# Output projection of a hybrid decoder block: eight half-size block products become seven, with block sums of rows and weights made on chip

## The chip, the cores and the metric

The kernel runs on one core of one Trainium2 chip. The metric is the device time of one execution in microseconds (us); lower is better. The engines are PE (matrix products, with PEld for the loading of its weights), DVE (vector), ACT (scalar, with the activation functions), POOL (GpSimd) and SP (which issues the DMA transfers). DVE and ACT read and write both memories on chip, SBUF and PSUM; POOL works on SBUF alone here; PE writes PSUM.

## What is computed

One layer of a decoder block on x of 1024 rows (sequence) by 1024 columns (model width), in float32:

```
h  = RMSNorm(x);  p = h @ w_in        # split into q, k, v, latents, gate_a, gate_b
A  = sliding-window attention          B = latent attention, causal
y  = sigmoid(gate_a) * (A @ w_o_swa) + sigmoid(gate_b) * (B @ w_o_mla)
x  = x + y @ w_out                     # the output projection: 1024 x 1024 by 1024 x 1024
h  = RMSNorm(x, ffn_norm_g)
x  = x + (silu(h @ w_gate) * (h @ w_up)) @ w_down
return RMSNorm(x, final_norm_g)
```

## The kernel before

**Precision.** Each factor of a product is split into a high part in the rounded matmul format fp32r and a low part, the rest. `split` (line 161) makes them: ACT copies to the high part (line 163), DVE subtracts it from the source (line 166). `mm3` (line 168) then issues three matmuls for each block of 128 of the inner dimension: high x high, high x low, low x high (lines 172, 173, 174), 512 columns wide, into one PSUM bank.

**Block products.** The gates (`gates`, 8 pairs of weight columns), the feed-forward's first products (`ffn`) and its last one already use seven products of half-size blocks instead of eight (class `Seven`, line 710): sums of blocks of both factors are made first, and the seven results are added up in two groups of PSUM banks, A (products 1, 2, then 5, 3) and B (6, 7, 4). `prep_to(n)` (line 784) converts weights up to the n-th product of the list, `run` (line 789) issues one product, after it has called prep_to for as many ahead as `n_ahead` says. The output projection still is eight half-size products, one after the other.

**Sliding-window stage** (lines 1025 to 1042). Sixteen iterations of attention are interleaved with the gates' products, three a piece: `gate_step`, transposes of q (`sw_qT`), `gate_step`, `sw_pv`, `sw_scores` of the next iteration (score products, maxima on DVE, exponentials on ACT), `gate_step`, `sw_pT`. The order on all engines is the order of the program here.

**Latent attention** (line 1360 on) carries in its slots the products A @ w_o_swa (`mix_a`, line 1276): result rows `ar`, in blocks dc of 128 of the model width. Those of dc 0 to 3 go out to memory (`ar_d`), those of dc 4 to 7 stay on chip.

**Mixing** (`mix_b`, line 1411, called from the loop at line 1444). For each dc in the order DCS = (4, 5, 0, 1, 6, 7, 2, 3) and each half of the sequence (`sh`, 512 columns): 12 matmuls with w_o_mla into a bank `oB`; DVE multiplies by the sigmoid of gate b (line 1420) and adds the product of gate a and `ar` that POOL made (lines 1434, 1426); `split` writes the row's parts into `quad` (`yh`, `yl`). y is held transposed: a block dc of it is 128 of the inner dimension of the next product. The loads and conversions of w_o_mla (`ob`) and of w_out (`out`) are set into the loop by hand through the list `st` (`load_to`, `conv_to`).

**Projection** (lines 1611 to 1652). Four segments (half of the sequence, half of the columns): (0,0), (0,1), (1,1), (1,0). In each, four row blocks b of 128; for each b 24 matmuls (8 blocks of the inner dimension in the order DCS, three each) into a bank `xo`, and DVE adds the bank to x (line 1629). When a row block is complete in both halves of the columns, its norm follows: Square with a sum on ACT (line 1635), mean and power on POOL (lines 311, 314), scaling on DVE (line 1640), and one block later `to_h` (line 1468): 8 transposes on PE and the block differences that the feed-forward's seven products need (for b 0 to 3 the blocks b11, b21; for b 4 to 7 t2, t3, b22, and later t1, t4, on DVE). The w_out weights of the third segment are loaded and converted anew, 12 units of 128 x 1024 in all.

**Feed-forward start** (lines 1653 to 1676). Eight products (q 1 and 2 of two pairs, for gate and up weights) need only b11 and b21; the ninth needs t2 of all four late row blocks.

**What sets the order.** Inside `tc.manual_schedule(...)` the named engines keep the order of the program. From line 1043 to the fourth segment of the projection no engine is held: there the framework orders each engine's instructions when the program is built, by their place in the program and by what it reckons to be ready; an instruction can be moved ahead of earlier ones that wait. From the fourth segment on (line 1613) PE, DVE, ACT and POOL are held. At run time each engine works strictly in its order. On-chip buffers are two pools: 21 of 4 KB a partition (`U`) and 17 of 8 KB (`V`); PSUM has 8 banks, 4 for `P1` and 4 for `PX`. A tile waits until a buffer of its pool is free.

## Time and profile before

| | |
|---|---|
| time, median of 3 runs | 1345.6 us (1345.04 to 1346.36) |
| time of the profiled execution | 1345.58 us |
| its span | 1343.8 us |
| mean granted clock of PE | 0.998 |
| DMA | 223.61 MB, mean 166 GB/s |

The profile is one execution, recorded by the hardware on the one core. Its views: the page (busy time of each engine and its costliest groups of instructions), the list of waits (who waited for whom: total, times, longest), the groups of one stretch ("x16 | 16.3, 1035 | 0.6" reads: 16 instructions, 16.3 us busy, 1035 ns the mean of one, 0.6 us idle on the engine just before them), the stretches (busy time of each engine between two times) and the timeline (start, duration, engine, line, operation, what it writes <- what it reads; in brackets the idle time of the engine before it and what ended that). Times are counted from the start of the span. Matmuls are pipelined: their durations overlap, and the cost of one is the distance between starts. Line numbers are those of the kernel before.

### The profile page before, as it was taken

How to read it: one execution, taken by the hardware profiler on the slowest of the kernel's cores; microseconds unless marked ns; L12 is line 12 of the kernel's file. 1: busy time of each engine (PE TensorE's matmuls, PEld its weight loads, DVE VectorE, ACT ScalarE, POOL GpSimd, SP SyncE). 2: the span in 40 equal slices, each digit the busy share in tenths (PEclk: the TensorE clock that was granted, in tenths of full speed). 3: DMA queues.
4: the chain of work that ended last, by engine and by line, in shares of the span. 5: the costliest groups of instructions: out<-in, count | busy, mean ns of one | idle time of the engine just before them, and what ended most of it. 6: DMA issues, size and time to landing. Idle time of an engine off the chain costs nothing. (4 is left out here: it accounts for less than half of the span.)

```text
span 1343.8 us, 19035 instructions
## 1 busy us (share of the span) xinstructions
PE 1325.5 (99%) x6564; PEld 1115.0 (83%) x6564; DVE 903.5 (67%) x1471; ACT 635.7 (47%) x1291; POOL 567.6 (42%) x614
## 2 busy tenths in 40 slices
...
GB/s 374 152 188 156 118 97 83 109 124 187 155 243 160 107 99 17 264 268 48 190 140 96 166 175 146 203 162 180 177 141 153 164 96 194 383 373 238 173 13 144
DMA packets 85311, 223.61 MB, mean 166 GB/s; under 512 B 9632, under 2 KB 16288, under 8 KB 84128
## 3 DMA queue, kind: packets, MB, share of 16 engines
...
q8 instruction: 52, 0.85, 0.3%
...
## 5 line engine op out<-in xcount | busy, mean ns | idle before, releaser
L166 DVE TENSOR_TENSOR wl<-wr,wl 128x512 fp32r<-128x512 f32 x150 | 150.8, 1029 | 72.6 <-ACT wl L163 72.2
L166 DVE TENSOR_TENSOR lrv<-lr,lrv 128x1024 fp32r<-128x1024 f32 x77 | 105.1, 1396 | 49.3 <-ACT lrv L163 45.3
L163 ACT CAST lrv<-lr 128x1024 fp32r<-128x1024 f32 x77 | 80.1, 1052 | 95.7 <-PE fd L174 69.8
L172 PE MATMUL fd<-lrv 128*128 128x512 f32 x308 | 119.8, 389 | 0.0
L173 PE MATMUL fd<-lrv 128*128 128x512 f32 x308 | 119.8, 389 | 0.0
L174 PE MATMUL fd<-lrv 128*128 128x512 f32 x308 | 119.8, 389 | 0.0
L177 POOL TENSOR_TENSOR wr<-wr,sm 128x512 f32<-128x512 f32 (+1 forms) x38 | 46.2, 1225 | 145.4 <-DVE wl L166 114.2
L163 ACT CAST wl<-wr 128x512 fp32r<-128x512 f32 x150 | 86.9, 622 | 1.9 <-DVE wr L835 1.7
L1198 POOL TENSOR_TENSOR denb<-denb,neg_one 128x1 f32<-128x1 f32 x64 | 40.1, 626 | 96.2 <-ACT p L1197 84.1
L166 DVE TENSOR_TENSOR wl<-sm,wl 128x512 fp32r<-128x512 f32 x60 | 48.7, 837 | 46.3 <-ACT wl L163 46.2
L311 POOL TENSOR_SCALAR ms<-ss 128x1 f32<-128x1 f32 x32 | 9.4, 292 | 143.7 <-ACT xn L1635 67.5
L173 PEld LDWEIGHTS fd<-lrv 128*128 128x128 f32 x308 | 57.8, 188 | 12.1
L174 PEld LDWEIGHTS fd<-lrv 128*128 128x128 f32 x308 | 57.8, 188 | 12.0
L172 PEld LDWEIGHTS fd<-lrv 128*128 128x128 f32 x308 | 57.8, 188 | 11.9
L1197 ACT ACTIVATE p<-scb,nmb 128x384 f32<-128x384 f32 (+3 forms) x64 | 47.8, 747 | 33.3 <-DVE nmb L1196 25.6
L166 DVE TENSOR_TENSOR ptl<-pTb,pth 128x512 fp32r<-128x512 f32 (+2 forms) x96 | 50.5, 552 | 16.6 <-ACT pth L163 16.3
L1196 DVE CUSTOM_DVE_ANT_0 scb<-scb,mask 128x384 f32<-128x384 f32 (+3 forms) x64 | 48.6, 761 | 15.0 <-PE scb L1188 13.0
L1529 ACT ACTIVATE act<-sm 128x512 f32<-128x512 f32 x11 | 7.0, 633 | 104.8 <-DVE sm L180 104.8
L1199 POOL TENSOR_SCALAR p<-p,denb 128x384 f32<-128x384 f32 (+3 forms) x64 | 47.9, 748 | 6.3
L172 PE MATMUL xo<-wv,yh 128*128 128x512 f32 x120 | 47.4, 395 | 1.2 <-ACT yh L163 1.2
L1529 ACT ACTIVATE act<-pu 128x512 f32<-128x512 f32 x22 | 13.9, 633 | 71.0 <-DVE pu L180 71.0
L163 ACT CAST pth<-pTb 128x512 fp32r<-128x512 f32 (+2 forms) x96 | 43.4, 482 | 8.5 <-PE pTb L1213 7.5
...
## 6 DMA issues: line engine op xcount, KB each, us to landing
...
```

Of the source, the lines that this page charges most:

```text
L163: i = nc.scalar.copy(hi, src)
L166: (eng or nc.vector).tensor_tensor(lo, src, hi.bitcast(F32), op=ALU.subtract)
L172: nc.tensor.matmul(ps, ah, bh, start=first and i == 0, stop=False, skip_group_check=go_on)
L173: nc.tensor.matmul(ps, ah, bl, start=False, stop=False, skip_group_check=go_on)
L174: nc.tensor.matmul(ps, al, bh, start=False, stop=last and i == n - 1, skip_group_check=go_on)
L177: eng.tensor_tensor(out, a, b, op=ALU.subtract)
L311: nc.gpsimd.tensor_scalar(ms, ss, 1.0 / width, EPS, op0=ALU.mult, op1=ALU.add)
L1196: nc.vector.tensor_tensor_reduce(s_, s_, m_, 1.0, -NEG, op0=ALU.add, op1=ALU.min, accum_out=nm)
L1197: nc.scalar.activation(p_, s_, AF.Exp, scale=-1.0, bias=nm, accum_out=den)
L1198: nc.gpsimd.tensor_tensor(den, den, neg_one[:, 0:1], op=ALU.pow)
L1199: nc.gpsimd.tensor_scalar(p[:, 0:w], p[:, 0:w], den, 0.0, op0=ALU.mult, op1=ALU.add)
L1529: nc.scalar.activation(dst, src, AF.Silu)
```

## The change

The projection becomes seven products of half-size blocks, in the order 1, 2, 6, 5, 3, 7, 4, with four row blocks b each and 12 matmuls for each b. With y and w_out cut into 2 x 2 blocks, the sums of y blocks (`y_sums`) are made in place on POOL, those of w_out (`w_sums`) on DVE, and each product's two factors are split when their turn comes (`split_left`, `conv_out`; `left` and `wop` hold them). The mixed rows stay on chip in float32 (`ya`) until their sums are made; only the blocks that enter a product unsummed are split inside `mix_b`. Partial results are copied by ACT (p1, p5) and added to x by DVE (`xo`) and POOL (`more`). PE keeps the order of the program from the first product on, all four engines from the seventh product in the list's order (q = 7) on. The four early row blocks are normed behind product 3, the four late ones behind product 4, which ends the projection. In `to_h` three of the late blocks' subtractions move from DVE to POOL. The two halves of the model width swap roles (dc 0 to 3 for 4 to 7) in `mix_a`, `ar_d` and DCS, and the w_o_mla weights go to the `V` pool. In the sliding-window stage, two calls of `prep_to` are added ahead of `sw_scores`.

```diff
@@ -296,15 +296,10 @@
     for k in range(2):
         ukv_unit(k)
     uq_unit(2)
-    for dp in range(4):
+    for dp in (2, 3, 0, 1):
         plain(("oa", dp), w_o_swa[dp], (P, 4, 256), True)
-    for dp in (2, 0, 3, 1):
-        plain(("ob", dp), w_o_mla[dp], (P, 4, 256))
-    OUT0 = (2, 0, 3, 1)
-    for r, hf in enumerate((0, 1, 0)):
-        for j in (range(4) if r else OUT0):
-            plain(("out", r, j), w_out[hf, j], (P, 2, 512), (r, j) != (2, 3))
-
+    for dp in (0, 2, 1, 3):
+        plain(("ob", dp), w_o_mla[dp], (P, 4, 256), True)
...
@@ -1032,6 +1027,8 @@
         if it >= 1:
             sw_pv(it - 1)
         if it + 1 < N_SW:
+            if gates.seq[gates.n_run][:2] in ((2, 1), (5, 1)):
+                gates.prep_to(gates.n_run + 3)
             sw_scores(it + 1)
         if it == N_SW - 1:
...
@@ -1308,14 +1305,14 @@
     wo = {}
     NT = NH * NB
     LATE = True
-    DCS = (4, 5, 0, 1, 6, 7, 2, 3)
+    DCS = (0, 1, 4, 5, 2, 3, 6, 7)
...
@@ -1408,23 +1405,63 @@
     if not LATE:
         mix_a(*rest.pop(0), 0, 4, PX("oA"))
+    left = {}
+    ya = {}
+    def new_left(q):
+        left[q] = (V("yh", F32R), V("yl", F32R))
     def mix_b(dc, i):
         if dc % 2 == 0:
             wo[4 + dc // 2] = st.get(("ob", dc // 2))
         w = wo[4 + dc // 2]
         ga, gb = gate.pop(dc), gate.pop(8 + dc)
+        ya[dc] = ga
         for sh in range(2):
             cs = half(sh)
             pb = PX("oB")
             mm3(pb, [((w[0][:, c, blk(dc % 2)], w[1][:, c, blk(dc % 2)]), obT[(c, sh)]) for c in range(4)])
             nc.vector.tensor_tensor(gb[:, cs], pb, gb[:, cs], op=ALU.mult)
-            if i == 7:
-                add(ga[:, cs], ga[:, cs], gb[:, cs], nc.vector)
-                split(*hT(dc, cs), ga[:, cs])
-        for sh in range(2 if i < 7 else 0):
-            cs = half(sh)
             add(ga[:, cs], ga[:, cs], gb[:, cs], nc.vector)
-            split(*hT(dc, cs), ga[:, cs])
+            if dc >= 4 or sh == 0:
+                hi, lo = left[1 if dc < 4 else 2 if sh == 0 else 4]
+                split(hi[:, dc % 4], lo[:, dc % 4], ga[:, cs])
+    def y_sums(k):
+        a, b = ya[k], ya[4 + k]
+        a_lo, a_hi, b_lo, b_hi = a[:, half(0)], a[:, half(1)], b[:, half(0)], b[:, half(1)]
+        add(b_hi, a_hi, b_hi, nc.gpsimd)
+        sub(a_hi, a_lo, a_hi, nc.gpsimd)
+        sub(a_lo, b_hi, a_lo, nc.gpsimd)
+        sub(b_lo, b_lo, a_lo, nc.gpsimd)
+    S_OF = {6: (0, 0), 7: (0, 1), 3: (1, 0), 5: (1, 1)}
+    def split_left(q):
+        new_left(q)
+        kh, sh = S_OF[q]
+        for k in range(4):
+            split(left[q][0][:, k], left[q][1][:, k], ya[4 * kh + k][:, half(sh)])
+    wraw = {}
+    wop = {}
+    def load_out(kh, hf, j):
+        wraw[(kh, hf, j)] = U("wr", F32, (P, 2, 512))
+        nc.sync.dma_start(wraw[(kh, hf, j)], w_out[hf, 2 * kh + j])
+    W_OF = {1: (0, 0), 2: (1, 0), 3: (1, 1), 4: (1, 0), 5: (0, 1), 6: (0, 0), 7: (1, 1)}
+    def conv_out(q, j, eng=None):
+        wop[(q, j)] = halves_of((P, 2, 512), True)
+        split(*wop[(q, j)], wraw[(*W_OF[q], j)], eng)
+    def w_sums(j, eng):
+        b11, b12, b21, b22 = (wraw[(kh, hf, j)] for kh in range(2) for hf in range(2))
+        sub(b22, b22, b12, eng)
+        sub(b12, b12, b11, eng)
+        add(b11, b11, b22, eng)
+        sub(b21, b21, b11, eng)
...
@@ -1439,13 +1476,16 @@
     held[0] = True
     sigmoids(DCS[0])
     held[0] = False
-    st.conv_to(st.index[("ob", 0)])
-    new_quads("y")
+    st.conv_to(st.index[("ob", 2)])
+    new_left(1)
     for i, dc in enumerate(DCS):
         if i in (1, 2):
-            st.load_to(st.index[("ob", (3, 1)[i - 1])])
-        if 2 <= i < 6:
-            st.load_to(st.index[("out", 0, OUT0[i - 2])])
+            st.load_to(st.index[("ob", i * 2 - 1)])
+        if 4 <= i:
+            load_out(0 if i < 6 else 1, 0, i % 2)
+        if i == 2:
+            new_left(2)
+            new_left(4)
         if i + 2 < 8:
             load_sigs(DCS[i + 2])
         if rest:
@@ -1454,23 +1494,25 @@
             sigmoids(DCS[i + 1])
         mix_b(dc, i)
         if i in (2, 3):
-            st.conv_to(st.index[("ob", (3, 1)[i - 2])])
-        if i >= 4:
-            st.conv_to(st.index[("out", 0, OUT0[i - 4])])
+            st.conv_to(st.index[("ob", 2 * i - 3)])
+        if i in (4, 5):
+            y_sums(i - 4)
+        if i in (5, 6):
+            conv_out(1, i - 5)
     fg_bc = bcast_gain("ffng", ffn_g)
     raw1 = {}
-    x2 = {}
     late = []
     hq.clear()
+    x2 = {}
     def to_h(xn, b):
         c = b % 4
         pss = []
         for kh in range(2):
-            ps = PX("tp", (P, 4, P))
+            ps = (P1 if b < 4 else PX)("tp", (P, 4, P))
             for j in range(4):
...
@@ -1492,16 +1534,18 @@
         nc.scalar.copy(t23[:, 1], pss[0])
         sub(t23[:, 0], pss[1], r[:, 0], nc.vector)
         nc.scalar.copy(hq["t2"][0][:, :, blk(c)], t23[:, 0])
-        sub(r[:, 1], r[:, 1], t23[:, 0], nc.vector)
+        hi, lo = hq["t2"]
+        sub(lo[:, :, blk(c)], t23[:, 0], hi[:, :, blk(c)].bitcast(F32), nc.gpsimd)
+        sub(r[:, 1], r[:, 1], t23[:, 0], nc.gpsimd)
         late.append((c, r))
         def rest():
             sub(t23[:, 1], pss[1], t23[:, 1], nc.vector)
             nc.scalar.copy(hq["b22"][0][:, :, blk(c)], pss[1])
             nc.scalar.copy(hq["t3"][0][:, :, blk(c)], t23[:, 1])
-            for name, src in (("t2", t23[:, 0]), ("b22", pss[1]), ("t3", t23[:, 1])):
+            for name, src in (("b22", pss[1]), ("t3", t23[:, 1])):
                 hi, lo = hq[name]
-                sub(lo[:, :, blk(c)], src, hi[:, :, blk(c)].bitcast(F32), nc.vector)
+                sub(lo[:, :, blk(c)], src, hi[:, :, blk(c)].bitcast(F32), nc.vector if name == "b22" else nc.gpsimd)
         return rest
...
@@ -1605,64 +1649,157 @@
             split_h(name, c, r[:, i])
         late[c] = None
+    pe_order = tc.manual_schedule(engines={engines.PE})
+    pe_order.__enter__()
+    p1, p5 = V("xp1"), V("xp5")
+    lo, hi = half(0), half(1)
+    bank = {}
+    normed = {}
+    def xo(q, b):
+        if q in (1, 6, 5):
+            bank[("B" if q == 6 else "A", b)] = (PX if q == 6 else P1)("xo")
+        ps = bank[("B" if q in (6, 7, 4) else "A", b)]
+        lh, ll = left[q]
+        mm3(ps, [((lh[:, k, blk(b)], ll[:, k, blk(b)]), (wop[(q, k // 2)][0][:, k % 2], wop[(q, k // 2)][1][:, k % 2]))
+                 for k in range(4)], first=q in (1, 6, 5), go_on=q in (2, 7, 4, 3))
+        if q == 1:
+            nc.scalar.copy(p1[:, b], ps)
+        elif q == 5:
+            nc.scalar.copy(p5[:, b], ps)
+        else:
+            x_ = x2[b if q in (2, 6, 3) else 4 + b][:, {2: lo, 6: hi, 3: hi, 7: hi, 4: lo}[q]]
+            add(x_, ps, x_, nc.vector)
+    def norm_a(b):
+        xn = U("xn")
+        ss = tiny("ss")
+        nc.scalar.activation(xn, x2[b], AF.Square, accum_out=ss)
+        normed[b] = xn, rstd_of(ss, D)
+    def norm_b(b):
+        xn, rs = normed[b]
+        nc.vector.scalar_tensor_tensor(xn, x2[b], rs, fg_bc, op0=ALU.mult, op1=ALU.mult)
+        nc.sync.dma_start(x2_d[b], x2.pop(b))
+    def more(x_, p):
+        add(x_, x_, p, nc.gpsimd)
+    conv_out(2, 0)
+    conv_out(2, 1)
+    for j in range(2):
+        load_out(0, 1, j)
+        load_out(1, 1, j)
+    y_sums(2)
+    y_sums(3)
+    for b in range(4):
+        xo(1, b)
+        if b == 0:
+            w_sums(0, nc.vector)
+        if b == 1:
+            w_sums(1, nc.vector)
+        if b == 2:
+            conv_out(6, 0)
+            split_left(6)
+        if b == 3:
+            conv_out(6, 1)
+        x2[b] = load_x(b)
+    for b in range(4):
+        xo(2, b)
+        more(x2[b][:, hi], p1[:, b])
+        if b == 1:
+            conv_out(5, 0)
+            split_left(5)
+        if b == 2:
+            conv_out(5, 1)
+    for b in range(4):
+        xo(6, b)
+        if b == 0:
+            for j in range(2):
+                wraw[(0, 0, j)] = None
+                t = wraw[(0, 0, j)] = U("wr", F32, (P, 2, 512))
+                nc.sync.dma_start(t, w_out[1, 2 + j])
+            W_OF[3] = (0, 0)
+        if b == 2:
+            split_left(3)
+            conv_out(3, 0)
+        if b == 3:
+            conv_out(3, 1)
+    for b in range(4):
+        xo(5, b)
+        if b == 0:
+            split_left(7)
+            conv_out(7, 0)
+        if b == 1:
+            conv_out(7, 1)
+        x2[4 + b] = load_x(4 + b)
+        more(p5[:, b], p1[:, b])
+    for b in range(4):
+        xo(3, b)
+        more(x2[4 + b][:, hi], p5[:, b])
+        more(x2[4 + b][:, lo], p1[:, b])
+        norm_a(b)
+        norm_b(b)
+        if b == 1:
+            conv_out(4, 0)
+        if b == 2:
+            conv_out(4, 1)
+    ffn.load_part(0, 0)
+    pe_order.__exit__(None, None, None)
     in_order = tc.manual_schedule(engines={engines.PE, engines.DVE, engines.Activation, engines.Pool})
...
+    in_order.__enter__()
+    for b in range(4):
+        xo(7, b)
+        if b == 0:
+            ffn.load_part(0, 1)
+        to_h(normed.pop(b)[0], b)
+        if b == 1:
+            ffn.mix(0)
+    ffn.prep_to(3)
+    lowers = {}
+    def to_h_of(b):
+        lowers[b] = to_h(normed.pop(b)[0], b)
     ffn.n_ahead = 1
...
+    xo(4, 0)
+    norm_a(4)
+    xo(4, 1)
+    norm_a(5)
+    norm_b(4)
+    xo(4, 2)
+    norm_a(6)
+    norm_b(5)
+    to_h_of(4)
+    xo(4, 3)
+    norm_a(7)
+    norm_b(6)
+    to_h_of(5)
+    for kh in range(2):
+        ffn.load_part(1, kh)
+    norm_b(7)
     ffn.run()
     ffn.prep_to(4)
...
+    to_h_of(6)
+    lowers.pop(4)()
+    ffn.run()
+    ffn.prep_to(5)
+    to_h_of(7)
+    lowers.pop(5)()
     ffn.run()
     ffn.prep_to(6)
...
+    lowers.pop(6)()
     ffn.run()
+    ffn.prep_to(8)
     ffn.run()
...
+    lowers.pop(7)()
     ffn.prep_to(8)
     for i in range(1, 6):
         if i == 2:
```

(Of the last piece only the new lines stand here; the old ones are lines 1608 to 1668 above.)

## Prediction, made before the changed kernel was run

> **What bounds the kernel now.** I read the page first, then PE's waits, then the stages around the output projection, then single rows.

> ```profile
> span 1343.8 us, 19035 instructions
> PE 1325.5 (99%) x6564; PEld 1115.0 (83%) x6564; DVE 903.5 (67%) x1471; ACT 635.7 (47%) x1291; POOL 567.6 (42%) x614
> ```

> The profiled execution took 1345.58 us, 1.8 more than its span, and the median of the three runs is 1345.6, so a sum against the execution holds for the median. PE is busy 99% of the span: a matmul removed is time gained, as long as nothing makes PE wait instead. PE's few waits, from the list of waits:

> ```profile
> PE fa L172 <- ACT wl L163: 3.3, 3, 1.5
> PE xo L172 <- ACT yh L163: 1.2, 1, 1.2
> PE oB L172 <- ACT wh L163: 0.9, 1, 0.9
> PE oB L174 <- DVE wl L166: 0.9, 1, 0.9
> ```

> All of these lie in stages that the diff touches. The stretches, whose columns are length, then PE, PEld, DVE, ACT and POOL busy, clock and DMA share, show how much room the other engines have:

> ```profile
> 564.00:588.00 24.00, 23.06 (x102) 18.80 (x101) 18.57 (x23) 15.22 (x19) 12.65 (x8) 1.00 0.71 249
> 588.00:610.00 22.00, 21.11 (x94) 17.14 (x93) 21.69 (x24) 16.00 (x19) 12.07 (x8) 1.00 0.91 342
> 610.00:632.00 22.00, 20.76 (x91) 16.57 (x90) 13.53 (x18) 6.21 (x8) 2.01 (x1) 1.00 0.00 1
> 632.00:660.00 28.00, 28.00 (x137) 23.42 (x136) 11.03 (x13) 9.04 (x18) 2.61 (x8) 1.00 0.17 70
> 660.00:683.00 23.00, 23.00 (x107) 19.12 (x106) 11.56 (x13) 7.43 (x11) 8.96 (x7) 1.00 0.73 281
> 705.00:731.00 26.00, 24.54 (x114) 19.81 (x113) 22.98 (x34) 17.45 (x32) 3.67 (x4) 1.00 0.34 116
> ```

> The gated mixing (mix_b) runs from 564 to 610, the projection (xo) from 610 to 705, then the feed-forward. In the second half of mix_b DVE has 0.3 of 22 us left: it is as full as PE. From 610 to 683 DVE and POOL are half empty. The change puts its new work there.

> **The matmuls.** The projection now:

> ```profile
> L172 PE MATMUL xo<-wv,yh x120: 389/389/497, 610.2 to 703.8; 128*128 128x512 f32 x120
> L172 PE MATMUL xo<-wh,yh x8: 389/389/389, 683.6 to 702.4; 128*128 128x512 f32 x8
> ```

> That is 128 of each of three kinds, 384 in all. Their 389 ns overlap; the cost of one is the step between starts. From the first row below to the second lie 18 steps: 4.08 / 18 = 0.2267 us.

> ```profile
> 610.16 0.39 PE L172 MATMUL xo<-wv,yh 128*128 128x512 f32 x1
> 614.24 0.39 PE L172 MATMUL xo<-wv,yh 128*128 128x512 f32 x1
> 616.32 0.50 PE L172 MATMUL xo<-wv,yh 128*128 128x512 f32 x1 [1.24 <-ACT yh L163]
> ```

> Seven products of 4 row blocks x 4 k blocks x 3 are 336: 48 fewer, 48 x 0.2267 = **-10.9 us**. The 64 transposes stay.

> **The gates.** Two of the three fa waits lie in the sliding-window stage:

> ```profile
> 190.85 0.58 ACT L964 COPY ot<-o 64x512 f32<-64x512 f32 x1
> 195.09 0.47 ACT L933 ACTIVATE pe<-sc,nm 128x256 f32<-128x256 f32 x1 [3.66 <-DVE nm L925]
> 197.00 0.62 ACT L163 CAST wl<-wr 128x512 fp32r<-128x512 f32 x1
> 197.68 0.50 PE L172 MATMUL fa<-hh,wl 128*128 128x512 f32 x1 [1.04 <-ACT wl L163]
> 276.76 0.50 PE L172 MATMUL fa<-hh,wl 128*128 128x512 f32 x1 [0.76 <-ACT wl L163]
> 277.83 0.39 PE L172 MATMUL fa<-hh,wl 128*128 128x512 f32 x1
> ```

> The weight cast for the matmul at 197.68 sits on ACT behind the exponentials, though ACT stood idle for 3.66 us before them. The new prep_to issues it ahead of the scores, into that hole. Behind it on DVE the score reductions come one subtract (0.69) later, on ACT the exponentials as much; the transposes that read them follow two gate products of 2.7 us later, so that costs nothing. Besides 1.04 + 0.76, each wait slows the three matmuls behind it: 1.07 us from 276.76 to 277.83 instead of 0.68, 0.39 each. I take 1.80 + 2 x 0.39, less 0.1 for the slow step that follows any transpose: **-2.5 us**; the bounds are 0 and -2.6.

> **The start of the projection.** The 1.24 us at 616.32 is the last mixed row's split, which the old order needs in the first row block. The first product now reads only rows 0 to 3 of the first half, made two passes of the loop before the end. 1.24 + 0.39 = **-1.6 us** (bounds 0 and -1.6). The two oB waits hang on the conversion of the third weight unit, which keeps its pass; its buffers move to the other pool. I leave them; bounds -2.3 (both vanish) and +1. That the mixed rows and their weights swap halves (0 to 3 for 4 to 7) changes no count and no place: 0.

> **New work on DVE and POOL up to the third product (q=6).** It is the first that needs sums of rows and weights; it starts 2 x 48 x 0.2267 = 21.8 us after mix_b ends, at 610.2 + 21.8 = 632.0, and its last k blocks are due 6 to 9 matmuls later, 1.6 us: 633.6. The prices:

> ```profile
> L180 DVE TENSOR_TENSOR sg<-sg,sg 128x512 f32<-128x512 f32 x16 | 16.3, 1035 | 0.6
> L166 DVE TENSOR_TENSOR yl<-sg,yh 128x512 fp32r<-128x512 f32 x16 | 13.0, 832 | 3.4 <-ACT yh L163 3.1
> L1420 DVE TENSOR_TENSOR sg<-oB,sg 128x512 f32<-128x512 f32 x16 | 10.8, 679 | 2.6 <-ACT sg L1269 2.6
> L166 DVE TENSOR_TENSOR wv<-wr,wv 128x1024 fp32r<-128x1024 f32 x5 | 7.0, 1403 | 0.0
> L166 DVE TENSOR_TENSOR wl<-wr,wh 128x1024 fp32r<-128x1024 f32 x3 | 4.1, 1383 | 0.0
> ...
> L1434 POOL TENSOR_TENSOR sg<-ar,sg 128x512 f32<-128x512 f32 x16 | 26.7, 1690 | 30.7 <-ACT sg L1269 23.0 <-DVE sg L180 7.7
> ```

> And the steps between starts:

> ```profile
> 569.58 1.21 DVE L166 TENSOR_TENSOR wl<-wr,wh 128x1024 fp32r<-128x1024 f32 x1
> 570.71 0.68 DVE L1420 TENSOR_TENSOR sg<-oB,sg 128x512 f32<-128x512 f32 x1
> ...
> 613.68 1.28 DVE L166 TENSOR_TENSOR yl<-sg,yh 128x512 fp32r<-128x512 f32 x2
> ```

> Undisturbed, a 128x512 operation on DVE takes 0.68 and the next starts after 0.60 (two in 1.28); a 128x1024 one takes 1.21 and a step of 1.13. The products that read PSUM stay at 0.68 whatever POOL does; those with both inputs in SBUF are longer when POOL works. Over mix_b the excess is 16 x (1.035 - 0.68) + 16 x (0.832 - 0.68) + 5 x (1.403 - 1.21) + 3 x (1.383 - 1.21) = 9.6 us for POOL's 16 products: c = 0.60 us of DVE lost for each POOL operation. The bounds on c are 0 (no overlap) and 1.1 (the longest yl in the tile's view, 1783 ns, against 0.68).

> From 588, where DVE stops having idle time, its list up to q=6 is, in 128x512 operations: 9 products, 9 adds, 8 splits (12 now instead of 16 in the loop), 4 splits of the row sums, 3 adds behind q=2; in 128x1024 operations: 2 weight units of mix_b, 6 converted weights for q=1, 2 and 6, 8 weight sums. 33 x 0.60 + 16 x 1.13 = 37.9 us of the 633.6 - 588 = 45.6. POOL has 8 products left, 16 row sums (y_sums) and 2 additions to x: 26 operations, so DVE ends 26c - 7.7 us too late. The three adds and two last weight sums are not needed by q=6; if the scheduler puts them behind, 1.8 + 2.3 less. At c = 0.60 the wait is 7.9 in written order and 3.8 at best: I take **+6.0 us**. POOL itself isn't late: its 30.7 us of idle time in mix_b cover two of the row sums (8 x 1.69 = 13.5), and the last ones start when DVE has made the last row, near 619, and are through their third step by 624.5 or 631 at 1.69 each.

> ACT gets 12 splits and 2 weights more, and is at 6.21 of 22 behind 610. SP issues 10 loads of w_out instead of 12; rows, weights, gain and x take 8 + 8 + 1 + 4 = 21 buffers, all there are, so the x loads go out only when the last gates are used up. The queues move nothing from 610 to 632 (share 0.00), and x is first read 13.6 us after mix_b: hidden.

> **From q=6 to the last product.** For q=6, 5 and 3 (32.7 us of PE) DVE has 12 splits, 9 adds, 6 weights and 3 norms: 21 x 0.60 + 6 x 1.13 + 3 x 1.28 = 23.2, plus 14 POOL additions x 0.60 = 8.4: 31.6. It fits by 1 us; I cost it at 0, bounds 0 and +4.

> **Start of the feed-forward.**

> ```profile
> 699.03 0.68 DVE L180 TENSOR_TENSOR x<-xo,x 128x512 f32<-128x512 f32 x1
> ...
> 699.88 1.06 ACT L1635 ACTIVATE xn<-x 128x1024 f32<-128x1024 f32 x1 [1.58 <-DVE x L180]
> ...
> 702.54 1.28 DVE L1640 SCALAR_TENSOR_TENSOR xn<-x,rstd,ffng 128x1024 f32<-128x1024 f32 x1 [0.72 <-ACT wl L163]
> ...
> 718.77 0.50 PE L172 MATMUL fa<-b11h,wl 128*128 128x512 f32 x1 [1.46 <-ACT wl L163]
> ```

> A late block's chain of add, square, power and scaling takes 702.54 + 1.28 - 699.03 = 4.8 us. Such a block came every 24 matmuls, 5.4 us; now one comes every 12, 2.7, plus about 0.9 of transposes. It asks of DVE 1 add, 4 subtracts and the scaling, 5 x 0.60 + 1.28 = 4.3, and three subtracts moved to POOL cost it 3c = 1.8: 6.1 against 3.6. Four blocks leave 10 us of work to the eight feed-forward products (8 x 2.72 = 21.8 us), which ask 0.60 of DVE each. That fits, but in an order written by hand. Before, PE waits 1.46 + 0.39 here; I take 1 us more, **+1.0**, bounds -1.9 and +4.

> **Sum.** -10.9 - 2.5 - 1.6 + 6.0 + 1.0 = -8.0; 1345.58 - 8.0 = **1337.6 us**.

> **Rivals.**
> 1. *No wait at q=6.* The scheduler fills POOL's and DVE's holes early enough, c stays below 0.45: 1337.6 - 6 = 1331.6. For it speaks that DVE has 8 us to spare without POOL; against it the 1.035 of the adds.
> 2. *The clock answers the wait.* The wait at q=6 is longer than any idle time of PE in this trace (1.46), and PE was slow when it started cold:

> ```profile
> 2.48 2.13 PE L510 MATMUL warm<-warm 128*128 128x512 bf16 x5
> ```

> Five starts in 2.13 - 0.43 are steps of 0.425, against 0.2267. Were some 15 matmuls of q=6 to run so, 15 x 0.2 = 3 us more: 1340.6. [...]
> 3. *The gain is eaten.* c = 0.85 makes the wait 14.4 in written order: 1346.0, no difference.
> 4. *Slower: DVE and POOL block each other from mix_b to q=6.* Gains and the feed-forward's +1 come to -14.0; slower by over 2.7 needs a wait over 16.7, so c over 0.94, or c over 0.82 with the clock's 3 us. At c = 1.0 the wait is 18.3 and with the clock 21.3: 1353. For it speaks that behind 599 nearly all of DVE's operations have two SBUF inputs; against it that a third of POOL's list can run before.
> 5. *The moved gate cast does nothing*, because its source isn't scaled by then: 1340.1.

> **Chances.** Forecast 0.32, rival 2 0.10, rival 1 0.23, rival 5 0.05: faster 0.70. Rival 3 0.13, rival 4 0.17. About 0.2%, 2.7 us, is what a measurement of this kernel can tell from no change. The range, 1329.5 to 1348, takes in rivals 1, 2, 3 and 5, and a bit of luck with the oB waits; it leaves out rival 4 and 0.03 below.

> **What would show it.** PE has 48 matmuls less on xo, at the same step. The rows at 197.68 and 276.76 have no wait. No wait at the first xo. One wait of some 6 us ahead of the third product, released by ACT or DVE splits of weight or row sums, with DVE without idle time before it and adds well over 0.68. The forecast fails if that wait is under 3 or over 10 us, if the feed-forward starts with more than 4 us of waits, or if mix_b itself grows by over 2 us.

## The result, and the profile after

The changed kernel takes **1361.5 us** (median of 4 runs, 1360.7 to 1361.9) beside 1345.3 for the kernel before on the same chip: ratio 1.0117, 95% interval 1.0103 to 1.0132. (The ratios, here and below, are not the quotients of the two medians and can differ a little from them.) I had forecast 1337.6, faster. The time went the other way by 16.2 us, 24 us from the forecast.

The head of the page after:

```profile
span 1359.8 us, 19029 instructions
PE 1326.4 (98%) x6516; PEld 1112.1 (82%) x6516; DVE 950.8 (70%) x1485; ACT 648.1 (48%) x1313; POOL 646.2 (48%) x658
```

The 48 matmuls are gone (6564 to 6516), yet the span is 16.0 us longer. DVE works 47 us more and POOL 79.

First, where it went. Each stage is taken from the start of its first matmul to the start of the next stage's first: oB for the mixed rows, xo for the projection, fa for the feed-forward, fb for its first product with late rows.

| stage | before, us | after, us | difference | forecast |
|---|---|---|---|---|
| start to first oB | 564.23 | 564.57 | +0.3 | -2.5 |
| mixed rows (oB to xo) | 45.93 | 49.83 | +3.9 | 0 |
| projection (xo to fa) | 95.08 | 100.87 | +5.8 | -6.5 |
| feed-forward's start (fa to fb) | 24.82 | 30.74 | +5.9 | +1.0 |
| rest of the span | 613.74 | 613.83 | +0.1 | 0 |

All of it lies between 564 and 746 us. The transposes of one row block, 0.9 us, have moved from the projection to the feed-forward's start: before, those of seven blocks ended ahead of the first fa, now those of six. PE's list of waits in 560 to 760 us of the kernel after:

```profile
PE xo L172 <- ACT xp L1667: 8.1, 2, 4.6
PE tp L1517 <- ACT t L1534: 2.7, 1, 2.7
PE tp L1517 <- DVE b11l L166: 2.7, 1, 2.7
PE oB L174 <- DVE wv L166: 2.5, 1, 2.5
PE tp L1517 <- DVE xn L1682: 1.6, 1, 1.6
PE oB L172 <- ACT wv L163: 1.6, 1, 1.6
PE tp L1517 <- DVE b22l L177: 1.3, 1, 1.3
```

These are 20.5 us, where the same stretch had some 4.5 before. The largest is not at product 6, where I had put the wait, but at product 2: it adds onto the bank of product 1, and ACT must first have copied that bank to xp (L1667). Products 6, 5 and 3 run without any wait.

ACT's rows at product 2:

```profile
627.85 0.62 ACT L163 CAST yh<-sg 128x512 fp32r<-128x512 f32 x1 [6.70 <-DVE sg L180]
630.06 1.04 ACT L163 CAST wv<-wr 128x1024 fp32r<-128x1024 f32 x1 [1.59 <-DVE wr L180]
631.01 0.58 ACT L1667 COPY xp<-xo 128x512 f32<-128x512 f32 x1
...
639.57 0.62 ACT L163 CAST yh<-sg 128x512 fp32r<-128x512 f32 x1 [6.43 <-POOL sg L177]
640.10 1.07 ACT L1667 COPY xp<-xo 128x512 f32<-128x512 f32 x2
```

The copies are short and their banks had long been ready. They stand in ACT's queue behind casts: of a mixed row, which waits 6.70 us for an add of DVE, of a weight unit, which waits 1.59 for a weight sum, and of a summed row, which waits 6.43 for a row sum of POOL. So one asks why DVE and POOL are late. The stretches (columns as in the prediction):

```profile
588.00:614.00 26.00, 23.39 (x95) 18.88 (x96) 25.55 (x22) 13.15 (x17) 23.79 (x14) 0.93 0.38 124
614.00:640.00 26.00, 18.66 (x75) 14.42 (x73) 25.91 (x20) 6.32 (x11) 18.42 (x10) 0.93 0.27 81
640.00:670.00 30.00, 29.27 (x117) 23.94 (x118) 30.00 (x31) 17.13 (x27) 16.16 (x10) 0.89 0.27 88
```

DVE is busy 25.55 of 26, 25.91 of 26 and 30.00 of 30 us, and yet it gets only 20 operations done from 614 to 640. The groups of DVE in 586 to 650 us tell why (count, then busy us and mean ns of one):

```profile
L166 DVE TENSOR_TENSOR wv<-wr,wv 128x1024 fp32r<-128x1024 f32 x9 | 16.2, 1807 | 0.0
L166 DVE TENSOR_TENSOR yl<-sg,yh 128x512 fp32r<-128x512 f32 x13 | 14.8, 1144 | 0.9 <-ACT yh L163 0.7
L177 DVE TENSOR_TENSOR wr<-wr,wr 128x1024 f32<-128x1024 f32 x6 | 12.1, 2023 | 0.0
L180 DVE TENSOR_TENSOR sg<-sg,sg 128x512 f32<-128x512 f32 x10 | 11.6, 1156 | 0.4
L1424 DVE TENSOR_TENSOR sg<-oB,sg 128x512 f32<-128x512 f32 x10 | 6.8, 678 | 0.0
L180 DVE TENSOR_TENSOR wr<-wr,wr 128x1024 f32<-128x1024 f32 x2 | 4.6, 2288 | 0.0
```

Only the product that reads PSUM (L1424) keeps its 0.68 us. Against 1.21 and 0.68 us undisturbed, the rest lost 9 x 0.60 + 13 x 0.46 + 6 x 0.81 + 10 x 0.48 + 2 x 1.08 = 23.2 us. POOL's groups in the same stretch:

```profile
L177 POOL TENSOR_TENSOR sg<-sg,sg 128x512 f32<-128x512 f32 x8 | 15.1, 1894 | 0.6
L1471 POOL TENSOR_TENSOR sg<-ar,sg 128x512 f32<-128x512 f32 x7 | 12.1, 1744 | 0.0
L177 POOL TENSOR_TENSOR sg<-sg 128x512 f32<-128x512 f32 x4 | 8.2, 2040 | 0.2
L180 POOL TENSOR_TENSOR x<-x,xp 128x512 f32<-128x512 f32 x4 | 7.9, 1985 | 0.0
L180 POOL TENSOR_TENSOR sg<-sg,sg 128x512 f32<-128x512 f32 x4 | 6.8, 1710 | 9.6 <-DVE yl L166 9.6
```

That is 27 operations: 23.2 / 27 = **0.86 us of DVE lost for each operation of POOL**, where I had taken 0.60. Single rows of DVE show the shape of it:

```profile
616.15 1.21 DVE L166 TENSOR_TENSOR wv<-wr,wv 128x1024 fp32r<-128x1024 f32 x1
...
619.87 2.31 DVE L177 TENSOR_TENSOR wr<-wr,wr 128x1024 f32<-128x1024 f32 x1
622.10 1.77 DVE L166 TENSOR_TENSOR yl<-sg,yh 128x512 fp32r<-128x512 f32 x1
```

From 614 to 619.4 POOL stood still, waiting for DVE, and the 128x1024 operation took 1.21 us. Beside POOL it took 2.31, and the 128x512 one 1.77 instead of 0.68: **1.10 and 1.09 us more, whatever the length**. (Other meetings cost less: 0.3 or 0.5 us.) So what DVE lost in these two was a fixed time and not a share of its own length; and the PSUM reader behind them, at 623.80 us, took its 0.68 with POOL at work all along.

The wait costs a second time. PE's rows at the third row block of product 2:

```profile
640.73 0.80 PE L172 MATMUL xo<-wv,yh 128*128 128x512 f32 x1 [4.58 <-ACT xp L1667]
641.33 0.63 PE L173 MATMUL xo<-wv,yh 128*128 128x512 f32 x1
641.75 0.63 PE L174 MATMUL xo<-wv,yl 128*128 128x512 f32 x1
...
646.45 0.44 PE L173 MATMUL xo<-wv,yh 128*128 128x512 f32 x1
```

Behind the wait of 4.58 us the step from matmul to matmul is 0.427 us until 646.45, then 0.23 again. The clock granted in the stretch is 0.89.

Would the copies alone, had they stood ahead of the casts, have saved this? The rows say no, as far as DVE's order stays as it is. Without the waits product 6 would start at 625.28 + 10.88 = 636.2 and need the low part of its second weight unit by 637.7; that unit's weight sum ends at 642.30, and DVE makes the low part from 647.35 to 648.56 at the earliest. The wait would have stood there, some 11 us long. No run moves the copies alone.

In product 7 the transposes wait for the normalised rows. DVE's rows there:

```profile
682.28 1.28 DVE L1682 SCALAR_TENSOR_TENSOR xn<-x,rstd,ffng 128x1024 f32<-128x1024 f32 x1 [2.18 <-POOL rstd L309]
683.49 0.68 DVE L180 TENSOR_TENSOR x<-xo,x 128x512 f32<-128x512 f32 x1
686.35 1.28 DVE L1682 SCALAR_TENSOR_TENSOR xn<-x,rstd,ffng 128x1024 f32<-128x1024 f32 x1 [2.19 <-POOL rstd L309]
```

DVE stands still for 2.18 us until block 0 has its rstd, with the add of block 1 behind it in the queue. Only after that add can the square and the rstd of block 1 begin, and DVE waits again. The four chains run one behind the other, in the order that the scheduler gave DVE.

### The profile page after: what moved, and what is told of

It is laid out like the page before. It is cut to its first block, busy times and chain, and to the rows that moved or that the text cites. A ratio compares the mean times of both kernels' runs of the same rounds, so it can differ in the third digit from the quotient of the medians.

```text
span 1359.8 us, 19029 instructions
## 1 busy us (share of the span) xinstructions
PE 1326.4 (98%) x6516; PEld 1112.1 (82%) x6516; DVE 950.8 (70%) x1485; ACT 648.1 (48%) x1313; POOL 646.2 (48%) x658
## 5 line engine op out<-in xcount | busy, mean ns | idle before, releaser
L166 DVE TENSOR_TENSOR wl<-wr,wl 128x512 fp32r<-128x512 f32 x150 | 155.7, 1061 | 71.0 <-ACT wl L163 70.6
L166 DVE TENSOR_TENSOR lrv<-lr,lrv 128x1024 fp32r<-128x1024 f32 x77 | 105.1, 1395 | 48.0 <-ACT lrv L163 46.8
L163 ACT CAST lrv<-lr 128x1024 fp32r<-128x1024 f32 x77 | 80.1, 1052 | 94.1 <-PE fd L174 75.1
L174 PE MATMUL fd<-lrv 128*128 128x512 f32 x308 | 119.8, 389 | 0.0
L172 PE MATMUL fd<-lrv 128*128 128x512 f32 x308 | 119.8, 389 | 0.0
L163 ACT CAST wl<-wr 128x512 fp32r<-128x512 f32 x150 | 87.0, 623 | 1.9 <-DVE wr L830 1.7
L166 DVE TENSOR_TENSOR wl<-sm,wl 128x512 fp32r<-128x512 f32 x60 | 50.2, 862 | 47.2 <-ACT wl L163 47.2
L174 PEld LDWEIGHTS fd<-lrv 128*128 128x128 f32 x308 | 57.8, 188 | 12.1
L172 PEld LDWEIGHTS fd<-lrv 128*128 128x128 f32 x308 | 57.8, 188 | 11.8
L166 DVE TENSOR_TENSOR ptl<-pTb,pth 128x512 fp32r<-128x512 f32 (+2 forms) x96 | 50.5, 551 | 16.6 <-ACT pth L163 16.3
L172 PE MATMUL xo<-wv,yh 128*128 128x512 f32 x112 | 46.3, 413 | 8.1 <-ACT xp L1667 8.1
L180 POOL TENSOR_TENSOR du<-du,xq 128x512 f32<-128x512 f32 x8 | 16.3, 2050 | 69.5 <-DMA lr<-in_w_down_dram 50.4
L163 ACT CAST pth<-pTb 128x512 fp32r<-128x512 f32 (+2 forms) x96 | 43.4, 482 | 8.5 <-PE pTb L1210 7.5
```

What stands on the lines that cost most here:

```text
L163: i = nc.scalar.copy(hi, src)
L166: (eng or nc.vector).tensor_tensor(lo, src, hi.bitcast(F32), op=ALU.subtract)
L172: nc.tensor.matmul(ps, ah, bh, start=first and i == 0, stop=False, skip_group_check=go_on)
L174: nc.tensor.matmul(ps, al, bh, start=False, stop=last and i == n - 1, skip_group_check=go_on)
L180: eng.tensor_tensor(out, a, b, op=ALU.add)
```

## The experiments

The theory: DVE was full from 588 us on, and what the change gave POOL took DVE's time, 0.7 to 0.9 us for each operation; the waits at product 2 are where that arrives. The rivals: the orders of the queues (ACT's copies, the weight sums ahead of the rows, the chains of the norms), the clock, and plain lack of DVE time. All times are medians; each was measured beside the kernel before, which took 1345.1 to 1346.2 in these comparisons (e3 has two runs, the others four to ten).

| run | us | ratio to before, 95% |
|---|---|---|
| e1 gate conversions alone | 1347.4 | 1.0010 (0.9999 to 1.0022) |
| e2 no row sums | 1348.1 | 1.0016 (1.0004 to 1.0027) |
| e3 weight sums behind the rows | 1362.0 | 1.0112 (1.0087 to 1.0137) |
| e4 PE kept warm | 1360.4 | 1.0097 (1.0079 to 1.0115) |
| e5 norms apart | 1356.6 | 1.0080 (1.0063 to 1.0097) |
| e6 last transposes later | 1362.8 | 1.0133 (1.0116 to 1.0149) |
| e7 row sums on DVE | 1355.0 | 1.0070 (1.0055 to 1.0085) |
| e8 no row sums, norms apart, transposes later | 1343.5 | 0.9986 (0.9976 to 0.9995) |
| e9 row sums on DVE, norms apart, no gate edit | 1348.6 | 1.0021 (1.0011 to 1.0030) |
| e10 product 4 third | 1364.3 | 1.0141 (1.0125 to 1.0158) |
| e11 before, with idle POOL adds | 1355.7 | 1.0075 (1.0060 to 1.0090) |
| e12 as e10, norms behind the copies | 1354.6 | 1.0062 (1.0049 to 1.0076) |
| e13 late rows' subtractions on DVE | 1365.2 | 1.0141 (1.0127 to 1.0155) |
| e14 e9 with e13's and e15's edits | 1352.4 | 1.0047 (1.0034 to 1.0060) |
| e15 e9 with four additions later | 1350.7 | 1.0038 (1.0025 to 1.0051) |

### What do the row sums cost?

**e2.** The four lines of y_sums are left out of the changed kernel, so products 6, 7, 3 and 5 multiply rows that were never summed:

```diff
-        add(b_hi, a_hi, b_hi, nc.gpsimd)
-        sub(a_hi, a_lo, a_hi, nc.gpsimd)
-        sub(a_lo, b_hi, a_lo, nc.gpsimd)
-        sub(b_lo, b_lo, a_lo, nc.gpsimd)
```

> The changed kernel without the 16 sums of mixed rows on POOL (y_sums is empty, so the products read rows that aren't summed). Theory 'traffic': DVE's operations with two SBUF inputs are long because POOL works beside them; without the row sums DVE's weight sums fall from 2.2 to about 1.3 us, mix_b from 49.8 to 46 us, and the two waits in the second product (8.1 us) go: 1361 to about 1345. Rival 'order': DVE's and ACT's queues stand wrongly whatever POOL does, the second product keeps most of its waits (over 4 us): 1355 or more.

It took 1348.1, 13.4 us less than the changed kernel: 13.4 / 16 = 0.84 us for each of the sixteen operations. Products 1, 2, 6, 5 and 3 follow each other in 10.88 us each. No wait for xo is left in its list from 560 to 760 us; what is left lies at the transposes and in the mixed rows, with these among it:

```profile
PE tp L1513 <- ACT t L1530: 2.7, 1, 2.7
...
PE oB L174 <- DVE wv L166: 1.0, 1, 1.0
```

The wait for DVE in the mixed rows also fell, from 2.5 to 1.0: it was the third weight unit's conversion beside POOL's first row sums. The 1.6 us on ACT's cast stayed, and so did a stretch at half pace behind them (granted clock 0.93 from 588 to 614 us): the mixed rows took 48.2 us in this trace.

**e7.** The same sixteen operations on DVE:

```diff
-        add(b_hi, a_hi, b_hi, nc.gpsimd)
...
+        add(b_hi, a_hi, b_hi, nc.vector)
...
```

> The sixteen row sums are made by DVE instead of POOL, nothing else is changed. Theory (the cost is that DVE and POOL slow each other down when both work on two operands: a weight sum of DVE takes 2.3 us beside POOL and 1.21 alone, a row sum of POOL 1.7 to 2.2 and 1.28 alone): DVE gains 16 x 0.68 = 10.9 us of work and loses about 8 x 1.1 us on the weight sums and some 5 on the rest, so its stretch from the mixed rows to product 6 gets no longer, and what stands behind it gets shorter: 1352 to 1357. Rival (plain throughput of DVE, which is at 25.6 of 26 us from 588 us on): DVE is 10.9 us later, and the waits at product 2 and 6 grow by half of it or more: 1364 to 1370.

1355.0: 6.6 us less than with POOL, though DVE now has sixteen operations more in a stretch in which it was full. Its groups in 586 to 650 us:

```profile
L166 DVE TENSOR_TENSOR yl<-sg,yh 128x512 fp32r<-128x512 f32 x19 | 15.0, 811 | 0.7 <-ACT yh L163 0.7
L166 DVE TENSOR_TENSOR wv<-wr,wv 128x1024 fp32r<-128x1024 f32 x10 | 13.3, 1326 | 0.0
...
L177 DVE TENSOR_TENSOR wr<-wr,wr 128x1024 f32<-128x1024 f32 x6 | 7.2, 1211 | 0.0
```

The weight sums take 1211 ns instead of 2023, the splits 811 instead of 1144. Against "DVE lacks the time", this speaks for the theory: sixteen operations of POOL cost 13.4 us (e2), and DVE's doing them itself 1355.0 - 1348.1 = 6.9. Not all of the gain is theirs, though. POOL's first addition of p1 lasts 20.8 us here, from 618.96 to 639.77, while DVE works without a pause at its undisturbed times; in the changed kernel such additions took 1.7 to 2.2 us, and DVE was slow beside them. The rival isn't quite dead, though: at product 6, where I had first put the wait, the first row block now takes 8.3 us instead of 2.7.

**e11.** The disputed price by itself, in the kernel before:

```diff
             add(ga[:, cs], ga[:, cs], gb[:, cs], nc.vector)
             split(*hT(dc, cs), ga[:, cs])
+            add(gb[:, cs], gb[:, cs], gb[:, cs], nc.gpsimd)
```

> The kernel before with nothing of the change in it, and fourteen POOL adds of 128x512 laid beside the mixed rows, each on a tile that is no longer read, so that nobody waits for their results. Theory (an operation of POOL on two operands takes DVE's time although neither waits for the other): DVE, busy for 21.7 of 22 us from 588 us to the first product, gets later by 0.6 to 1 us for each add that falls beside it, and the first product starts 3 to 10 us later: 1348 to 1355. Rival (the engines are independent, what cost the changed kernel time was the waits for POOL's results): within 1 us of 1345.3.

1355.7, 10.0 us slower: 0.72 us for each of fourteen adds whose result nobody reads. DVE's groups over the same operations as those that the prediction counts (566 to 630 us, as all of it comes later):

```profile
L166 DVE TENSOR_TENSOR yl<-sg,yh 128x512 fp32r<-128x512 f32 x16 | 19.3, 1226 | 3.1 <-ACT yh L163 2.8
L180 DVE TENSOR_TENSOR sg<-sg,sg 128x512 f32<-128x512 f32 x16 | 15.7, 993 | 1.8 <-POOL sg L1435 1.2
L166 DVE TENSOR_TENSOR wv<-wr,wv 128x1024 fp32r<-128x1024 f32 x5 | 9.4, 1871 | 0.0
L166 DVE TENSOR_TENSOR wl<-wr,wh 128x1024 fp32r<-128x1024 f32 x3 | 3.9, 1293 | 0.0
```

The splits went from 832 to 1226 ns and the conversions wv from 1403 to 1871; the adds (L180) and wl are a little shorter than before, 993 beside 1035 and 1293 beside 1383. Over the undisturbed times this is 16 x 0.55 + 16 x 0.31 + 5 x 0.66 + 3 x 0.08 = 17.3 us, where the prediction had 9.6 without the adds: 7.7 us, or 0.55 of DVE for each add. The other 2.3 us are about what PE loses at half pace in this run (12 matmuls with a step of 0.43, 2.4 us). The gates' products, which POOL makes in the same queue, also come later by the adds ahead of them, so not all of the lengthening need cost time by itself; but DVE has no idle time from 590 to 620 us, so it didn't wait for them there. The rival, engines that don't disturb each other, is out.

**e3.** The weight sums behind the last mixed row's subtraction in DVE's queue:

```diff
-            w_sums(0, nc.vector)
+            with tc.issue_after(last_row[0]):
+                w_sums(0, nc.vector)
...
```

> The changed kernel with the eight weight sums issued on DVE behind the last mixed row's subtraction, so that no weight sum stands ahead of a mixed row that ACT's queue waits for. Theory 'order': the two waits in the second product (8.1 us and the slow matmuls behind them, about 4) go; the third product then waits for the weight sums by 4 to 8 us: 1353 to 1357. Theory 'traffic' alone: DVE has the same work, the wait only changes its place, within 2 us of the changed kernel: 1359.5 to 1363.

1362.0, no change. Product 2 has one wait of 6.3 us instead of two of 8.1 together, and the matmuls get 1.9 us of waits for converted weights that were not there:

```profile
PE xo L172 <- ACT xp L1668: 6.3, 1, 6.3
```

Here the order of DVE's queue decided where the wait stands and hardly how long it is.

### Does the clock cost anything?

**e4.** Thirteen and seventeen matmuls on an unused bank, ahead of the two row blocks of product 2 that wait:

```diff
     for b in range(4):
+        if b in (1, 2):
+            keep_warm({1: 13, 2: 17}[b])
         xo(2, b)
...
```

> The changed kernel with 13 and 17 idle matmuls, written to a bank that nobody reads, ahead of the second and third row block of the second product, where PE waits 3.5 and 4.6 us. Theory 'clock': the matmuls behind the two waits start every 0.427 instead of 0.227 us because PE was idle; kept busy they don't, and the time falls by about 4 us to 1357.5. Rival: the slow steps have another cause (late weights or banks): they stay, and the time is that of the changed kernel within 1 us.

1360.4; from the first oB to the first fb it takes 179.0 us instead of 181.4. The waits end when they did, but the third row block's matmuls then have their step of 0.23. Product 2 takes 21.1 us instead of 23.8, and product 6 then 0.9 more. So the clock's part of the loss there is some 2 to 2.7 us; what ran before the last wait ended was hidden in it. It is read from one trace of each kernel: the medians are only 1.1 us apart, and the intervals of the two ratios overlap. The theory's 4 us were too many.

### The norms in product 7

**e5.** The four xn behind the last add of product 3:

```diff
         norm_a(b)
-        norm_b(b)
...
+    for b in range(4):
+        with tc.issue_after(adds[(3, 3)]):
+            norm_b(b)
```

> Only the order of DVE's queue in the fifth and sixth product is changed: the normalised rows xn of row blocks 0 to 3 are issued behind all four adds of product 3, where the changed kernel has add, xn, add, xn, add, add, xn, xn, each xn having waited 2.18, 2.19, 1.58 and 0.72 us for POOL's rstd with the next block's add behind it. Theory (the norms are late because one chain stands behind the other in DVE's queue, not because DVE has too much to do): the stretch of product 7 with its transposes, 19.05 us in the changed kernel where 4 x 2.72 + 4 x 0.9 = 14.5 would do, loses 2.5 to 4.5 us, and the time falls to 1357 to 1359. Rival (DVE is full there, so that the order moves nothing): 1361 to 1362, with the transposes' waits kept.

1356.6: 5.0 us less, and product 7 with its transposes takes 14.6 us instead of 19.05. DVE's rows:

```profile
683.30 1.29 DVE L1683 SCALAR_TENSOR_TENSOR xn<-x,rstd,ffng 128x1024 f32<-128x1024 f32 x1 [0.39 <-POOL rstd L309]
685.31 1.28 DVE L1683 SCALAR_TENSOR_TENSOR xn<-x,rstd,ffng 128x1024 f32<-128x1024 f32 x1 [0.72 <-POOL rstd L309]
```

Block 0's xn even starts a microsecond later than before (683.30 beside 682.28), but the others follow every 2.0 us instead of after 4.1, 4.1 and 2.0. This loss was a matter of order alone.

### The gates

**e1.** The kernel before with the two early prep_to calls and nothing else:

```diff
         if it + 1 < N_SW:
+            if gates.seq[gates.n_run][:2] in ((2, 1), (5, 1)):
+                gates.prep_to(gates.n_run + 3)
             sw_scores(it + 1)
```

> The kernel before with only the two added prep_to calls ahead of sw_scores. The prediction's step: both waits for the weight cast (1.04 and 0.76 us, with the slow matmuls behind them 2.5) go, 1343.1 us. Rival, read off the changed kernel's trace: the casts of q queue behind the same exponentials on ACT, and the score products wait for them 0.8 us in the same two places, with slow matmuls behind: between -0.5 and +1 us, 1345 to 1346.5.

Ratio 1.0010: no gain. Its waits between 130 and 330 us:

```profile
PE sc L917 <- DVE qs L901: 1.6, 2, 0.8
PE fa L172 <- ACT wl L163: 0.6, 1, 0.6
```

The two fa waits of 1.8 us that I had seen are gone (the 0.6 is at another product, and the changed kernel doesn't have it). In their place the next scores wait twice for the split of q, which ACT and DVE now make behind the exponentials that the cast has delayed.

### The start of the feed-forward

**e6.** The transposes of row block 7 one product later:

```diff
     ffn.prep_to(5)
-    to_h_of(7)
     lowers.pop(5)()
     ffn.run()
     ffn.prep_to(6)
+    to_h_of(7)
     lowers.pop(6)()
```

> Only the transposes of row block 7 go behind the third product of the feed-forward instead of the second, which gives row blocks 4 and 5 time to free their banks. Theory (the stretch from the feed-forward's first product to its first late one, 30.74 us against 24.82 before, is long because the four banks are shared by row blocks whose last parts come later): the waits of those transposes, 2.7 us on the copy t and 1.3 us on b22l, go, with the slow matmuls behind them, and the time falls by 3 to 5 us to 1356.5 to 1358.5. Rival (DVE and POOL are late with everything there, and the wait goes to the next product's weights or to the late rows themselves): within 1 us of 1361.5.

1362.8: no gain. The waits on t and b22l went, and others came, so that product 4 and the feed-forward's start together take 45.3 us as in the changed kernel; the list from 700 us on:

```profile
PE tp L1517 <- DVE xn L1682: 2.8, 1, 2.8
PE fa L172 <- ACT pu L807: 2.0, 1, 2.0
```

**e13.** The three subtractions of each late row block back on DVE:

```diff
-        sub(lo[:, :, blk(c)], t23[:, 0], hi[:, :, blk(c)].bitcast(F32), nc.gpsimd)
-        sub(r[:, 1], r[:, 1], t23[:, 0], nc.gpsimd)
+        sub(lo[:, :, blk(c)], t23[:, 0], hi[:, :, blk(c)].bitcast(F32), nc.vector)
+        sub(r[:, 1], r[:, 1], t23[:, 0], nc.vector)
...
-                sub(lo[:, :, blk(c)], src, hi[:, :, blk(c)].bitcast(F32), nc.vector if name == "b22" else nc.gpsimd)
+                sub(lo[:, :, blk(c)], src, hi[:, :, blk(c)].bitcast(F32), nc.vector)
```

> The changed kernel with the three subtractions of each late row block (4 to 7) back on DVE, which the change had moved to POOL; nothing else differs. Theory (the feed-forward's start is 5.9 us longer for the same reason as product 2: twelve POOL operations on two operands beside a DVE that has 21.5 of 30 us to do): the stretch from the feed-forward's first product to its first late one falls from 30.74 us by 2 to 5, and the time to 1356.5 to 1359.5. Rival (the stretch is long because the late blocks' chains of add, square, power, scaling, transposes, copies come too close behind each other, whoever makes the subtractions): within 1.5 us of 1361.5.

1365.2, 3.6 us slower by the medians (the intervals of the two ratios just overlap), of which 1.6 are in the stretch that the edit touches. My theory fails here: the stretch from fa to fb takes 32.4 us instead of 30.7, and the wait for b22l, 1.3 in the changed kernel, is now

```profile
PE tp L1517 <- DVE b22l L177: 3.4, 1, 3.4
```

In this stretch DVE isn't full (21.5 of 30 us), it is late in a chain of short steps, and POOL takes steps off that chain; that is how I read it. What an operation of POOL takes from DVE cost time at product 2, where DVE had none left (25.91 of 26 us from 614 to 640), and none that shows here.

### All together, and what is left

**e8.** e2, e5 and e6 in one.

> The row sums are left out altogether (products 3, 5, 6 and 7 multiply the plain mixed rows), and the two edits of the other runs, norms apart and last transposes later, are both in. Theory (each of the three places has a loss of its own): the 1348.1 without the row sums falls by a further 2.5 to 4.5 and 3 to 5 us, to 1339 to 1343, which is under the kernel before. Rival (a wait that is taken away only comes back at the next place, as when the weight sums were put behind the rows): 1346 to 1349.

1343.5, 1.9 us under the kernel before and half a microsecond above the theory's range: 4.7 less than e2, which is e5's part; e6's gives nothing here either (30.2 us from fa to fb, 30.0 in e2). So even without any row sums, the change has 1.9 us left of the 14 that I had counted without the wait at product 6; the feed-forward's start alone, 30.2 us beside 24.8 before, takes 5.4.

**e9.** The full computation with e7's and e5's edits, and without the gates' edit:

> The full computation: the changed kernel with the row sums on DVE, the normalised rows of blocks 0 to 3 issued behind the four adds of product 3, and without the gate conversions moved ahead. Theory (three places, each with its own loss): the 6.6 and 5.0 us that the first two brought alone add up, and about 0.7 us comes for the gates: 1349 to 1350.5. Rival (both edits only empty the same queue of DVE, so that they overlap): 1352 to 1355.

1348.6, 12.9 us less than the changed kernel: the two gains, 6.6 and 5.0, add up. DVE is busy for 82.0 of the 82 us from 588 to 670, and the first row block of product 6 takes 8.4 us.

**e15.** e9, with the four additions of p1 to x behind product 6 instead of in product 2:

```diff
     for b in range(4):
         xo(2, b)
-        more(x2[b][:, hi], p1[:, b])
...
         xo(5, b)
+        with tc.issue_after(adds[(6, 3)]):
+            more(x2[b][:, hi], p1[:, b])
```

> The full computation: the run with sums on DVE and norms apart (1348.6), with only the four additions of p1 to x put behind product 6. Theory: 2.8 to 3.4 us of the 6.7 at product 6, so 1345 to 1346. Rival (DVE is as full in product 5, so that the four additions cost there what they cost here, as a later wait): 1348 to 1349.

1350.7, above both forecasts. Product 6 took 3.0 us less, as 4 x 0.7 to 0.86 would have it; but product 7 with its transposes took 5.0 more (21.2 us beside 16.2), on

```profile
PE tp L1515 <- DVE xn L1681: 4.9, 1, 4.9
```

And the 3.0 us are not DVE's: from 618 to 650 us its operations are 1.7 us over their undisturbed times in e9 and 2.4 here. PE waits 1.0 us less there, and the rest is the clock, 0.91 in e9 from 632 to 650 us and 1.00 here. DVE is full in both and comes to its first xn at 674.75 in e9 and at 675.77 here; PE, which is there earlier, waits the longer. So this run doesn't bear out the price of an addition. It shows that a wait which goes at one place comes back at the next as long as DVE's list is no shorter.

**e14.** e15 with e13's edit too.

> The full computation: the run with sums on DVE and norms apart (1348.6), with two more things taken out of POOL's way: the late blocks' three subtractions on DVE, and the four additions of p1 to x behind product 6 instead of beside DVE's backlog in product 2. Theory (each POOL operation beside a full DVE costs 0.7 to 0.86 us): four additions give 2.8 to 3.4 us of the wait at product 6, the subtractions 2 to 4 at the feed-forward: 1341 to 1344, under the kernel before. Rival (the additions only meet DVE later, in product 5, and the feed-forward's start doesn't depend on POOL): 1347 to 1349.

1352.4, 1.7 above e15, in the direction of e13; single runs of the two overlap.

**e10 and e12.** Product 4, whose rows need no sums, runs third in banks of its own (ACT copies it, POOL adds it), and product 7 last:

```diff
+    for b in range(4):
+        xo(4, b)
...
-    xo(4, 0)
-    norm_a(4)
-    xo(4, 1)
...
```

> The full computation, as in the run with sums on DVE and norms apart, with the products in another order: product 4, whose rows need no sums, runs third in banks of its own and is copied by ACT and added by POOL, then come 6, 5, 3, and 7 last, with the transposes of row blocks 0 to 3; row blocks 4 to 7 are transposed among the first six products of the feed-forward. Theory (with the sums on DVE the 5.5 us at product 6 are backlog: DVE works without a pause from 587 to 650 us and the first row sums are needed 10.9 us too early): 10.9 us more time ahead of product 6 removes that wait and the slow matmuls behind it, 5 to 7 us below the run with both edits: 1342.5 to 1345. Rival (the weight sums, of which product 4 needs all eight, are as late as the row sums were, and the wait moves to product 4; or the four row blocks behind product 7 are late for the feed-forward): 1347 to 1351.

1364.3. Products 4, 6, 5 and 3 ran in 10.9 to 11.3 us each, so the wait at product 6 was indeed a matter of 10.9 us. But the feed-forward's first product waited 12.4 us for its weights (fa, for ACT's cast wl). I had put ACT's squares of blocks 4 to 7 ahead of the copies of the transposes; one of them waited for POOL's rstd, behind weight sums. e12 puts them behind (against e10):

```diff
-        norm_a(4 + b)
         to_h(normed.pop(b)[0], b)
         if b >= 1:
-            norm_b(3 + b)
-        if b == 1:
-            ffn.mix(0)
-    ffn.prep_to(3)
+            norm_a(3 + b)
+        if b >= 2:
+            norm_b(2 + b)
+            ffn.prep_to({2: 1, 3: 3}[b])
...
```

> The run with product 4 third once more, with one order changed: in the last product the squares of row blocks 4 to 7 go behind ACT's copies of the transposes and the first three weight conversions of the feed-forward, and POOL's weight sums for the feed-forward behind its rstd. There, at 706 us, ACT's square waited for POOL's rstd with the copies and conversions behind it, and the feed-forward's second product waited 12.4 us for its weights. Theory (the order of the products did what was expected of it, since products 4, 6, 5 and 3 ran without a wait, and the whole of the rest was this one queue): 12.4 us and the slow matmuls behind it go, 1349 to 1351.5, and if the 3.5 and 1.2 us waits in the feed-forward go with it, 1344 to 1347. Rival (row blocks 4 to 7 are simply too late behind product 7, with all their copies, differences and conversions on ACT and DVE among the first feed-forward products): 1353 to 1358.

1354.6: 9.7 us less, in the rival's range. From oB to fb it takes 167.1 us (165.8 before), but from fb to fd 403.5 instead of 397.1, with a wait of 3.55 us for DVE at the second fb product: I take it that four late row blocks among the feed-forward's first products are too much for ACT and DVE. None of the full versions beats the kernel before; e9 comes nearest, at 1.0021.

## Why the prediction was wrong, point by point

- **The matmuls, -10.9: right.** 48 are gone and the step is the same; in e2 five products run at 10.88 us. PE's own work fell as forecast.
- **The first xo wait, -1.6: right.** Product 1 runs 10.88 us without a wait.
- **The gates, -2.5: wrong, at the bound of 0.** The step "that costs nothing" failed. I followed the delayed exponentials to the transposes that read them, and not to the next split of q in the same queues (e1). Rival 5 had the number (no gain) but not the reason: the casts did come early and their two waits went.
- **The oB waits, 0 with bounds -2.3 and +1: wrong, +3.9.** The conversion of the third unit came to lie beside POOL's first row sums; 1.6 us of that wait go when they do (e2). Another 1.6 us is the half pace behind the waits (8 steps of 0.427). Whether it comes is luck: e2 and e8 have the same two waits, 1.6 and 1.0 us, and from 580 to 600 us the clock is 0.91 in e2 and 1.00 in e8, where the mixed rows take 46.6 us. I had costed POOL's operations only for the list up to product 6, and not for a wait that already stood in the stretch.
- **The wait at product 6, +6.0: this term failed.** Its mechanism was right and its size and place were wrong. The price c = 0.60 us of DVE for each operation of POOL was too small: it was 0.86 in that stretch (by time, 0.84 for each row sum left out, waits and clock included). The 0.60 was an average over a stretch in which DVE had 0.3 to 5.4 us of room and POOL's operations often met a PSUM reader or nothing. Only the rows from 588 to 612 us, where DVE was full, give 7 x 0.51 + 6 x 0.12 + 4 x 0.24 + 2 x 0.26 = 5.8 us for POOL's 8 operations, or 0.72: the same trace, read where the new work was to go, would have made the wait 11 us. My bound of 1.1 was what a full meeting costs. With 0.86 the formula 26c - 7.7 gives 14.7 us; product 2 lost 12.9, clock included. The row sums account for it: without them it loses nothing (e2). But c is no constant: e11 has 0.55, and in e7 DVE lost nothing to an addition that POOL couldn't finish for 20.8 us. As for the place, I had followed the operands of the matmuls and not the bank: product 2 needs ACT's copy of product 1, and ACT's queue stood behind casts that waited for DVE and POOL. With the copies in time the wait would have stood at product 6 after all, as it does in e7.
- **From product 6 to the last, 0 with bounds 0 and +4: wrong.** Products 6, 5 and 3 fit, by 1 us or not. Product 7 lost 4.5 us, and 4.5 go when the norms stand in another order (e5); I had added them up as work and not laid them out as a chain. Product 4 lost some 1.8.
- **The feed-forward's start, +1.0: too small by 4.0** (of the 5.9 measured, 0.9 is the row block whose transposes have moved there). I had the chain of 4.8 us and the closer spacing of 2.7 us, and judged by DVE's sum that it fits. It is the chain that counts. Neither the place of row block 7's transposes (e6) nor POOL's share (e13) is the cause; that it is the spacing of the four chains is what remains, and no run shows it by itself.
- **The clock, rival 2: right as a mechanism**, 2 to 2.7 us at product 2 (e4), beside 3 that I had given it. No run shows the 15 matmuls of that estimate: behind the waits of 3.48 and 4.58 us there, 7 and 13 ran at the step of 0.427.
- **Rival 4**, DVE and POOL block each other, was what happened: I had let it begin at c over 0.82 with the clock's 3 us, gave it 1353 and 0.17. Its number came nearest, but partly by luck: its wait with the clock, 21.3 us, is 8.4 above the 12.9 at product 2, and what it left out is some 17: the mixed rows (3.9), products 7 and 4 (6.3), the feed-forward's start (4.0) and the gates (2.5).
